# One-hot rows written one token and key at a time, and the low weight parts of the expert products' first factor made on VectorE

## The chip, the core and the metric

The kernel runs on one core of a Trainium2 chip. The metric is the time of one execution on the device in microseconds. A core has TensorE (PE in the profile, its weight loads PEld), VectorE (DVE), ScalarE (ACT), GpSimd (POOL) and the queue that starts the plain DMA transfers (SP).

## What is computed

The reference is a decoder trunk of two layers over 512 tokens of width 1024. Layer 0 mixes tokens with chunkwise retention, layer 1 with causal differential attention. After each mixer, with a layer norm on either side, stands a PEER feed-forward block, and the change lies in that block. There each of 8 heads picks the best 16 of 128x128 = 16384 experts for each token, and the token's result is a sum over these 128 experts:

```python
s1, i1 = lax.top_k(sc[:, :, 0], PEER_TOPK)
s2, i2 = lax.top_k(sc[:, :, 1], PEER_TOPK)
cand = (s1[..., :, None] + s2[..., None, :]).reshape(PEER_CHUNK, PEER_HEADS, ncand)
cidx = (i1[..., :, None] * PEER_N_KEYS + i2[..., None, :]).reshape(PEER_CHUNK, PEER_HEADS, ncand)
top, pos = lax.top_k(cand, PEER_TOPK)
idx = jnp.take_along_axis(cidx, pos, axis=-1).reshape(PEER_CHUNK, PEER_HEADS * PEER_TOPK)
gate = jax.nn.softmax(top, axis=-1).reshape(PEER_CHUNK, PEER_HEADS * PEER_TOPK)
u_e = jnp.take(u, idx, axis=0)
v_e = jnp.take(v, idx, axis=0)
act = jax.nn.gelu(jnp.einsum('ted,td->te', u_e, xc).astype(jnp.float32))
return jnp.einsum('te,ted->td', (gate * act).astype(v_e.dtype), v_e)
```

## The kernel before

Tokens stand in four blocks of 128. In the PEER block, `peer`, block 0 is done sparsely: for each of its 128 picks a gather on GpSimd's queue fetches one row of u (`sparse_u`, line 752) and later of v (`sparse_v`, line 765) for every token, and VectorE takes the dot product (line 754, tile `scr`) or the weighted sum (line 767). Blocks 1 to 3, 384 tokens, are done densely: all 16384 experts are computed, as 128 tiles `a` of 128 experts, and multiplied with a gate matrix that is zero where an expert was not picked.

Every float32 product with the wide weights is made of three products of rounded parts (`mm3`, lines 107 to 109). `wload` brings a weight tile of 128x1024 in (`wraw`, a ring of 9 buffers that the gathered rows share), ScalarE copies it to its high part `wh` (line 103), and the subtraction on line 104 makes the low part `wl`, on the engine that the caller names and on VectorE if it names none.

`u_tile` is the first product of a dense tile: 24 matmuls of 384 columns, then gelu on ScalarE into `uact`. Its low part is made on GpSimd. `v_prep` and `v_mm` are the second product: 18 matmuls of 512 columns. Their low parts, `wl` of v and `wwl`, are made on VectorE.

The gate matrix comes from `gmat`. For four tokens at a time it builds two sets of one-hot rows of 128 keys, `g_oh`, one of them weighted with the gate, and PE multiplies them (line 844). One instruction on VectorE compares the number row with the keys of the four tokens in bf16 (line 837, `g_eq`, 1024 columns), ScalarE copies one half of the result to float32 (line 839), and VectorE multiplies the other half with the gate (line 840, 512 columns). There are 96 such groups of four tokens to a layer. `gate_rows` (lines 814 to 824, and the transposes of line 820) prepares the keys of a block of tokens, and `topk_pairs` (lines 695 to 739, tiles `tk_...`) picks the experts.

In a layer the order is: queries and scores with the first pick (`topk_keys`); `topk_pairs` for blocks 0 and 1; then `gates()`, which interleaves the gate groups of blocks 1 to 3, the picking of blocks 2 and 3, 82 of the 128 first products (their `uact` is stored to memory by SP) and part of the sparse dot products; then all 128 second products, of which the first 82 read `uact` back and the last 46 make their first product there, four ahead. The sparse rows of v are gathered in this last part. Fixed numbers (`UT`, `DOTS`, `LAG`, `PC`, and the costs that `gmat` yields) set the interleaving in program order, and the build's scheduler then sets the order on each engine. Each engine runs its own list in order.

Of the kernel before, what the change touches and what calls it, by code (L numbers as in the profile page):

```python
# [19 lines left out]
F32 = mybir.dt.float32  # L20
F32R = mybir.dt.float32r
BF16 = mybir.dt.bfloat16
I32 = mybir.dt.int32
U32 = mybir.dt.uint32
AF = mybir.ActivationFunctionType
OP = mybir.AluOpType
# [3 lines left out]
P = 128  # L30
# [22 lines left out]
VB = 4  # L53
NG0 = 2
OHB = 4
EQB = 2
UT = 4.0
RING = 9
SB = 4
# [4 lines left out]
def build(tc, I, out):  # L64
    nc = tc.nc
    ctx = ExitStack()
    with ctx:
# [8 lines left out]
        def ct(name, shape, dt=F32):  # L76
            return const.tile(shape, dt, name=name)
# [2 lines left out]
        mhalf = ct("mhalf", [P, 16])  # L80
        nc.vector.memset(mhalf, -0.5)
        iota50 = ct("iota50", [P, NCAND, 16], BF16)
        iota4 = ct("iota4", [P, P, 4], BF16)

        X = [xp.tile([P, D], F32, name=f"x{t}") for t in range(TB)]
        XTH = xp.tile([P, KD, S], F32R, name="xth")
# [724 lines left out]
        def gate_rows(kp, idx, gate):  # L811

            ii = kp.tile([P, 2, P], I32, name="g_ii", tag="g_ii")
            nc.vector.tensor_scalar(out=ii[:, 0, :], in0=idx, scalar1=7, scalar2=None, op0=OP.arith_shift_right)
            nc.vector.tensor_scalar(out=ii[:, 1, :], in0=idx, scalar1=127, scalar2=None, op0=OP.bitwise_and)
            fi = kp.tile([P, 2, P], F32, name="g_if", tag="g_if")
            nc.vector.tensor_copy(out=fi, in_=ii)
            b = bank("rt")
            for i, src in enumerate((fi[:, 0, :], fi[:, 1, :], gate)):
                nc.tensor.transpose(b[:, i * P:i * P + P], src, ident)  # L820
            tr = kp.tile([P, 3, P], F32, name="g_tr", tag="g_tr", bufs=2)
            nc.vector.tensor_copy(out=tr.rearrange("p a b -> p (a b)"), in_=b[:, :3 * P])
            ks = kp.tile([P, 2, P], BF16, name="g_ks", tag="g_ks", bufs=2)
            nc.vector.tensor_copy(out=ks, in_=tr[:, 0:2, :])
            return tr, ks

        def gmat(kp, tr, ks, t0, gd, G0):

            for q in range(P // GT):
                st = kp.tile([P, P - GA * NG0, GT], F32, name="g_st", tag="g_st", bufs=2)  # L830
                for r in range(GT // 4):

                    eq = kp.tile([P, 2, P, 4], BF16, name="g_eq", tag="g_eq", bufs=EQB)
                    oh = kp.tile([P, 2, 4, P], F32, name="g_oh", tag="g_oh", bufs=OHB)
                    tk = q * GT + r * 4
                    ts = slice(tk, tk + 4)
                    nc.vector.tensor_tensor(out=eq, in0=iota4[:, None].to_broadcast([P, 2, P, 4]),
                                            in1=ks[:, :, None, ts].to_broadcast([P, 2, P, 4]), op=OP.is_equal)
                    nc.scalar.activation(oh[:, 1], eq[:, 1].rearrange("p a t -> p t a"), AF.Copy)
                    nc.vector.tensor_tensor(out=oh[:, 0], in0=eq[:, 0].rearrange("p a t -> p t a"),  # L840
                                            in1=tr[:, 2, ts].unsqueeze(2).to_broadcast([P, 4, P]), op=OP.mult)
                    b = bank("pj")
                    for i in range(4):
                        nc.tensor.matmul(b[:, i * P:i * P + P], oh[:, 1, i, :], oh[:, 0, i, :], start=True, stop=True)  # L844
                    b3 = b.rearrange("p (t a) -> p t a", t=4)
                    rs = slice(r * 4, r * 4 + 4)
                    nc.scalar.activation(st[:, :, rs].rearrange("p a t -> p t a"), b3[:, :, GA * NG0:], AF.Copy)
                    for i in range(NG0):
                        nc.scalar.activation(G0[i][:, t0 // GT + q, :, rs].rearrange("p a t -> p t a"),
                                             b3[:, :, GA * i:GA * i + GA], AF.Copy)  # L850
                nc.sync.dma_start(gd[t0 // GT + q], st.rearrange("p a t -> p (a t)"))
                yield 6.0

        def u_tile(dp, l, a, tag="mu"):
            uh, ul = wload(I[f"ut{l}"][a], nc.gpsimd)
            b = bank(tag)
            for k in range(KD):
                newest["mm"] = mm3(b[:, :DT], uh[:, k, :], ul[:, k, :], XTH[:, k, S - DT:], XTL[:, k, S - DT:], k == 0, k == KD - 1)
# [20 lines left out]
        def peer(l, norm, feed, prepare):  # L879
            with tc.tile_pool(name="sp", bufs=1) as sp, tc.tile_pool(name="dp", bufs=1) as dp:  # L880
# [6 lines left out]
                with tc.tile_pool(name="p1", bufs=1) as kp:  # L887
                    M = [kp.tile([P, 16, 16], F32, name=f"tk_m{t}") for t in range(TB)]
                    MI = [kp.tile([P, 16, 16], U32, name=f"tk_i{t}") for t in range(TB)]
                    with tc.tile_pool(name="pq", bufs=1) as qp:  # L890
                        scores(qp, M, MI, l, norm, feed)
                        if l == 0:
                            iota_f = qp.tile([P, P], F32, name="iota_f")
                            nc.sync.dma_start(iota_f, I["iota"])
                            nc.vector.tensor_copy(out=iota50,
                                                  in_=iota_f[:, :NCAND].unsqueeze(2).to_broadcast([P, NCAND, 16]))
                            nc.vector.tensor_copy(out=iota4, in_=iota_f.unsqueeze(2).to_broadcast([P, P, 4]))
                    with tc.tile_pool(name="tk", bufs=1) as tp:
                        def pairs(t, got):
                            idx = tp.tile([P, P], I32, name="tk_idx", tag="tk_idx", bufs=2)  # L900
# [4 lines left out]
                        def gates():  # L905
# [18 lines left out]
                            for t in range(1, TB):  # L924
                                now = nxt
                                more = pairs(t + 1, got) if t + 1 < TB else ()
                                for n, cost in enumerate(gmat(tp, *now, (t - 1) * P, gd, G0)):
                                    yield cost
                                    for c in (more if n == P // GT - 4 else itertools.islice(more, 2)):
                                        yield c  # L930
# [158 lines left out]
```

## Time and profile before

| | us |
|---|---|
| median of 3 runs (3371.23 to 3378.87) | 3378.38 |
| the profiled execution | 3379.12 |
| its span | 3377.4 |
| VectorE busy in it | 2614.1 |
| GpSimd busy in it | 1604.4 |
| ScalarE busy in it | 1395.6 |

The granted clock of TensorE was 0.982 of full speed over the span. Times in the profile are of one execution. A row by line gives, after the count, the busy time of the group, the mean duration of one instruction, and the idle time of the engine before them with what ended it. Records of neighbouring VectorE instructions overlap a little: the next one starts before the end of the last is recorded. A duration holds the time for which an instruction that was already issued is kept from running.

For the stretches that the text speaks of: the picking of blocks 0 and 1 runs from about 545 to 655 us in layer 0 and from 2160 to 2268 us in layer 1; the gate stretch from 655 to 1003 and from 2268 to 2598 us; the second products with stored first products from 1003 to 1352 and from 2598 to 2960 us; the last stretch, with first products made there, from 1352 to 1690 and from 2960 to 3315 us.

### The profile page before, as it was taken

The numbers are of one execution on the slowest core, as the hardware profiler recorded it, in microseconds if no ns is written. First come the engines' busy times: TensorE is split into PE (matmuls) and PEld (weight loads), VectorE is DVE, ScalarE is ACT, GpSimd is POOL, SyncE is SP. The second block draws the span as 40 slices with busy tenths as digits, with TensorE's granted clock in tenths as the row PEclk, the third lists the DMA queues.
The fourth block names the chain that finished last, engine by engine and source line by source line (L and its number), as shares of the span: only waits on it lengthen the run. The fifth ranks groups of instructions, "written<-read, shape, count | busy, mean of one in ns | idle before, by whom it ended". The sixth has DMA issues, their size and how long they took to land.

```text
span 3377.4 us, 47027 instructions
## 1 busy us (share of the span) xinstructions
PE 3223.7 (95%) x16666; PEld 2852.8 (84%) x16666; DVE 2614.1 (77%) x4593; ACT 1395.6 (41%) x2436; POOL 1604.4 (48%) x919
## 2 busy tenths in 40 slices
PE   9999999799999999999999999989999999998998
PEld 7888889799998887888888668989999888788887
DVE  4444459999878888999973565899987887898896
ACT  3233333356673333333333543335677333333232
POOL 1101335655562333778734423565555323377782
PEclk9999999899999999999999999989999999999999
DMA  5222223467789999899942202336678999988893
GB/s 210 87 83 83 89 94 129 144 216 242 234 313 364 354 338 343 318 331 343 327 157 92 69 26 94 129 131 225 227 243 296 363 355 339 360 314 321 314 327 146
DMA packets 312637, 774.38 MB, mean 229 GB/s; under 512 B 25936, under 2 KB 154320, under 8 KB 312400
## 3 DMA queue, kind: packets, MB, share of 16 engines
q1 hardware_dynamic: 238672, 502.89, 43.4%
q0 software_dynamic: 73728, 268.47, 22.1%
q8 instruction: 131, 2.15, 0.3%
q14 instruction: 106, 0.87, 0.1%
HBM read 692.88 MB, written 78.38 MB: 228 GB/s over the span
## 4 chain that ended last, share of the span: by engine, by line
PE 60%; DVE 14%; issue 10%; POOL 7%; DMA 6%; ACT 2%; POOLq 0%; SPq 0%; DVEq 0%; ACTq 0%
PE pj L108 11%; PE pj L107 11%; PE pj L109 11%; PE rt L108 5%; PE rt L107 4%; PE rt L109 4%; POOL vg L765 3%; POOL wl L104 3%; PE mu L109 3%; PE mu L107 3%; PE mu L108 3%; PE pj L844 2%; DMA wraw<-in_ut 2%; DMA ug<-in_u,idx 2%; DVE tk_idf L736 2%
## 5 line engine op out<-in xcount | busy, mean ns | idle before, releaser
L104 POOL TENSOR_TENSOR wl<-wraw,wh 128x1024 fp32r<-128x1024 f32 x316 | 836.0, 2650 | 631.2 <-ACT wh L103 601.4
L103 ACT ACTIVATE wh<-wraw 128x1024 fp32r<-128x1024 f32 x632 | 660.4, 1054 | 592.3 <-PE pj L109 107.0
L104 DVE TENSOR_TENSOR wl<-wraw,wh 128x1024 fp32r<-128x1024 f32 x316 | 422.6, 1339 | 194.7 <-ACT wh L103 184.3
L752 POOL DMA_INDIRECT ug<-in_u,idx x256 | 325.1, 1270 | 477.9 <-DVE act L754 229.6
L109 PE MATMUL mu<-xth,wl 128*128 128x384 f32 (+1 forms) x1424 | 483.0, 339 | 22.6 <-POOL wl L104 22.5
L107 PE MATMUL mu<-xth,wh 128*128 128x384 f32 (+1 forms) x1424 | 482.9, 339 | 13.8 <-ACT wh L103 11.7
L108 PE MATMUL mu<-xtl,wh 128*128 128x384 f32 (+1 forms) x1424 | 479.6, 337 | 0.0
L765 POOL DMA_INDIRECT vg<-in_v,idx x256 | 338.1, 1321 | 168.1 <-DVE x L767 70.4
L754 DVE CUSTOM_DVE_ANT_0 scr<-ug,x 128x1024 bf16<-128x1024 f32 x256 | 354.6, 1385 | 57.9 <-DMA ug<-in_u,idx 57.1
L108 PE MATMUL pj<-wl,wwh 128*128 128x512 f32 x1024 | 398.8, 390 | 0.4 <-DVE wl L104 0.4
L767 DVE SCALAR_TENSOR_TENSOR x<-vg,wgt,x 128x1024 f32<-128x1024 f32 x256 | 394.4, 1541 | 4.4 <-DMA vg<-in_v,idx 1.2
L109 PE MATMUL pj<-wh,wwl 128*128 128x512 f32 x1024 | 396.6, 389 | 0.0
L103 ACT ACTIVATE wwh<-w 128x384 fp32r<-128x384 f32 x256 | 134.0, 525 | 633.6 <-PE rt L108 273.5
L107 PE MATMUL pj<-wh,wwh 128*128 128x512 f32 x1024 | 339.5, 393 | 19.4 <-ACT wh L103 17.4
L109 PEld LDWEIGHTS mu<-xth,wl 128*128 128x128 f32 x1424 | 270.8, 190 | 32.8 <-POOL wl L104 30.9
L107 PEld LDWEIGHTS mu<-xth,wh 128*128 128x128 f32 x1424 | 271.8, 191 | 21.0 <-ACT wh L103 13.7
L108 PEld LDWEIGHTS mu<-xtl,wh 128*128 128x128 f32 x1424 | 271.2, 190 | 3.1
L104 DVE TENSOR_TENSOR wwl<-w,wwh 128x384 fp32r<-128x384 f32 x256 | 171.3, 670 | 115.6 <-ACT wwh L103 114.9
L107 PEld LDWEIGHTS pj<-wh,wwh 128*128 128x128 f32 x1024 | 191.0, 188 | 60.2 <-ACT wh L103 22.6
L107 PE MATMUL rt<-xth,wh 128*128 128x384 f32 (+1 forms) x688 | 232.4, 338 | 0.2
L108 PE MATMUL rt<-xtl,wh 128*128 128x384 f32 (+1 forms) x688 | 230.6, 335 | 0.4 <-DVE xtl L104 0.4
L109 PE MATMUL rt<-xth,wl 128*128 128x384 f32 (+1 forms) x688 | 230.1, 334 | 0.0
(242 smaller groups left out, 6545.4 us busy)
## 6 DMA issues: line engine op xcount, KB each, us to landing
wraw<-in_ut SPq DMA_DIRECT2D x256, 512.0 KB, 4.6
wraw<-in_v SPq DMA_DIRECT2D x256, 512.0 KB, 7.0
gd<-g_st SPq DMA_DIRECT2D x48, 896.0 KB, 4.6
gl<-gd SPq DMA_DIRECT2D x28, 1536.0 KB, 14.0
ad<-uact SPq DMA_DIRECT2D x164, 192.0 KB, 2.9
aact<-ad SPq DMA_DIRECT2D x164, 192.0 KB, 6.5
wraw<-in_w_in SPq DMA_DIRECT2D x48, 512.0 KB, 4.0
wraw<-in_peer_w_q SPq DMA_DIRECT2D x32, 512.0 KB, 4.1
```

The source lines that it names most:

```text
L103: nc.scalar.activation(h, src, AF.Copy)
L104: newest["low"] = (eng or nc.vector).tensor_tensor(out=l, in0=src, in1=h.bitcast(F32), op=OP.subtract)
L107: nc.tensor.matmul(o, ah, bh, start=start, stop=False)
L108: nc.tensor.matmul(o, ah, bl, start=False, stop=False)
L109: return nc.tensor.matmul(o, al, bh, start=False, stop=stop)
L736: nc.vector.reduce_sum(out=idf[:, hs, :], in_=ex.rearrange("p h c k -> p h k c"), axis=AX.X)
L752: nc.gpsimd.indirect_dma_start(out=u, out_offset=None, in_=I[f"u{l}"], in_offset=bass.IndirectOffsetOnAxis(ap=idx[:, j:j + 1], axis=0))
L754: nc.vector.tensor_tensor_reduce(out=scr, in0=u, in1=X[t], scale=1.0, scalar=0.0, op0=OP.mult, op1=OP.add, accum_out=act[:, j:j + 1])
L765: nc.gpsimd.indirect_dma_start(out=v, out_offset=None, in_=I[f"v{l}"], in_offset=bass.IndirectOffsetOnAxis(ap=idx[:, j:j + 1], axis=0))
L767: nc.vector.scalar_tensor_tensor(out=X[t], in0=v, scalar=w[:, j:j + 1], in1=X[t], op0=OP.mult, op1=OP.add)
L844: nc.tensor.matmul(b[:, i * P:i * P + P], oh[:, 1, i, :], oh[:, 0, i, :], start=True, stop=True)
```

## The change

Two edits. In `gmat`, the two comparing and multiplying instructions on VectorE and the copy on ScalarE go. In their place come eight instructions on VectorE for each four tokens, each over 128 float32 columns of one token and one key: the number row is compared with that token's key, given as an operand of one value for each partition, and for the first key also multiplied with the token's gate, a second such operand. The tiles `g_eq` and `g_ks` and the number row in bf16 go. In `u_tile`, the low part is made on VectorE in place of GpSimd, for all 128 tiles of a layer.

```diff
--- before.py
+++ after.py
@@ -53,7 +53,6 @@
 VB = 4
 NG0 = 2
 OHB = 4
-EQB = 2
 UT = 4.0
 RING = 9
 SB = 4
@@ -80,7 +79,7 @@
         mhalf = ct("mhalf", [P, 16])
         nc.vector.memset(mhalf, -0.5)
         iota50 = ct("iota50", [P, NCAND, 16], BF16)
-        iota4 = ct("iota4", [P, P, 4], BF16)
+        iota = ct("iota", [P, P])
 
         X = [xp.tile([P, D], F32, name=f"x{t}") for t in range(TB)]
         XTH = xp.tile([P, KD, S], F32R, name="xth")
@@ -820,25 +819,22 @@
                 nc.tensor.transpose(b[:, i * P:i * P + P], src, ident)
             tr = kp.tile([P, 3, P], F32, name="g_tr", tag="g_tr", bufs=2)
             nc.vector.tensor_copy(out=tr.rearrange("p a b -> p (a b)"), in_=b[:, :3 * P])
-            ks = kp.tile([P, 2, P], BF16, name="g_ks", tag="g_ks", bufs=2)
-            nc.vector.tensor_copy(out=ks, in_=tr[:, 0:2, :])
-            return tr, ks
-
-        def gmat(kp, tr, ks, t0, gd, G0):
+            return tr
+
+        def gmat(kp, tr, t0, gd, G0):
 
             for q in range(P // GT):
                 st = kp.tile([P, P - GA * NG0, GT], F32, name="g_st", tag="g_st", bufs=2)
                 for r in range(GT // 4):
 
-                    eq = kp.tile([P, 2, P, 4], BF16, name="g_eq", tag="g_eq", bufs=EQB)
                     oh = kp.tile([P, 2, 4, P], F32, name="g_oh", tag="g_oh", bufs=OHB)
                     tk = q * GT + r * 4
-                    ts = slice(tk, tk + 4)
-                    nc.vector.tensor_tensor(out=eq, in0=iota4[:, None].to_broadcast([P, 2, P, 4]),
-                                            in1=ks[:, :, None, ts].to_broadcast([P, 2, P, 4]), op=OP.is_equal)
-                    nc.scalar.activation(oh[:, 1], eq[:, 1].rearrange("p a t -> p t a"), AF.Copy)
-                    nc.vector.tensor_tensor(out=oh[:, 0], in0=eq[:, 0].rearrange("p a t -> p t a"),
-                                            in1=tr[:, 2, ts].unsqueeze(2).to_broadcast([P, 4, P]), op=OP.mult)
+                    for i in range(4):
+                        key1, key2, gate = [tr[:, x, tk + i:tk + i + 1] for x in range(3)]
+                        nc.vector.tensor_scalar(out=oh[:, 1, i, :], in0=iota, scalar1=key2, scalar2=None,
+                                                op0=OP.is_equal)
+                        nc.vector.tensor_scalar(out=oh[:, 0, i, :], in0=iota, scalar1=key1, scalar2=gate,
+                                                op0=OP.is_equal, op1=OP.mult)
                     b = bank("pj")
                     for i in range(4):
                         nc.tensor.matmul(b[:, i * P:i * P + P], oh[:, 1, i, :], oh[:, 0, i, :], start=True, stop=True)
@@ -852,7 +848,7 @@
                 yield 6.0
 
         def u_tile(dp, l, a, tag="mu"):
-            uh, ul = wload(I[f"ut{l}"][a], nc.gpsimd)
+            uh, ul = wload(I[f"ut{l}"][a])
             b = bank(tag)
             for k in range(KD):
                 newest["mm"] = mm3(b[:, :DT], uh[:, k, :], ul[:, k, :], XTH[:, k, S - DT:], XTL[:, k, S - DT:], k == 0, k == KD - 1)
@@ -890,11 +886,9 @@
                     with tc.tile_pool(name="pq", bufs=1) as qp:
                         scores(qp, M, MI, l, norm, feed)
                         if l == 0:
-                            iota_f = qp.tile([P, P], F32, name="iota_f")
-                            nc.sync.dma_start(iota_f, I["iota"])
+                            nc.sync.dma_start(iota, I["iota"])
                             nc.vector.tensor_copy(out=iota50,
-                                                  in_=iota_f[:, :NCAND].unsqueeze(2).to_broadcast([P, NCAND, 16]))
-                            nc.vector.tensor_copy(out=iota4, in_=iota_f.unsqueeze(2).to_broadcast([P, P, 4]))
+                                                  in_=iota[:, :NCAND].unsqueeze(2).to_broadcast([P, NCAND, 16]))
                     with tc.tile_pool(name="tk", bufs=1) as tp:
                         def pairs(t, got):
                             idx = tp.tile([P, P], I32, name="tk_idx", tag="tk_idx", bufs=2)
@@ -924,7 +918,7 @@
                             for t in range(1, TB):
                                 now = nxt
                                 more = pairs(t + 1, got) if t + 1 < TB else ()
-                                for n, cost in enumerate(gmat(tp, *now, (t - 1) * P, gd, G0)):
+                                for n, cost in enumerate(gmat(tp, now, (t - 1) * P, gd, G0)):
                                     yield cost
                                     for c in (more if n == P // GT - 4 else itertools.islice(more, 2)):
                                         yield c
```

The scheduler's order of the two programs differs from the end of the scores on. (Lines are one to seven lower in the kernel after.) On VectorE in the gate stretch, before, a pair of picking steps, two instructions of a gate group and a sparse dot product (`scr`) stand like this:

```order
L744 TENSOR_REDUCE tk_z<-tk_g 128x8
L840 TENSOR_TENSOR g_oh<-g_eq,g_tr 128x512
L745 RECIPROCAL tk_z<-tk_z 128x8
L837 TENSOR_TENSOR g_eq<-iota_76,g_ks 128x1024
L746 TENSOR_TENSOR tk_g<-tk_g,tk_z 128x128
L840 TENSOR_TENSOR g_oh<-g_eq,g_tr 128x512
L837 TENSOR_TENSOR g_eq<-iota_76,g_ks 128x1024
```

In the kernel after, VectorE's list in the gate stretch reads:

```order
L834 TENSOR_SCALAR g_oh<-iota,g_tr 128x128
L836 TENSOR_SCALAR g_oh<-iota,g_tr 128x128
L103 TENSOR_TENSOR wl<-wraw,wh 128x1024
L753 ISA scr,act_3191<-ug,x_77 128x1024
L753 ISA act_3191 128x1
L729 TENSOR_TENSOR tk_eq<-iota_75,tk_pb 128x1600
L103 TENSOR_TENSOR wl<-wraw,wh 128x1024 x2
```

The one-hot instructions now stand in runs of alternating kinds, and the low parts of the first products (`wl`) stand between them. Of a layer's 82 low parts that are made ahead of the second products, 50 stand between the first and the last one-hot instruction, 23 in the picking of blocks 0 and 1 and eight ahead of it.

On GpSimd the low parts go from its list: between the query weights' parts at a layer's start and the last norms, the 128 gathers of u rows and then the 128 of v rows stand there behind one another, where before the low parts stood between them.

On PE, before, the gate matmuls stand in fours at the start of the gate stretch, each four behind one wait for VectorE's and ScalarE's halves:

```order
L844 MATMUL pj<-g_oh 128x128 [waits DVE_49,Activation_49]
L844 MATMUL pj<-g_oh 128x128 x3
L109 MATMUL mu<-xth,wl 128x384
L107 MATMUL mu<-xth,wh 128x384
L108 MATMUL mu<-xtl,wh 128x384
```

After, they stand there one by one between the matmuls of the first products:

```order
L840 MATMUL pj<-g_oh 128x128 [waits DVE_49] x2
L106 MATMUL rt<-xth,wh 128x384
L840 MATMUL pj<-g_oh 128x128 [waits DVE_49]
L107 MATMUL rt<-xtl,wh 128x384
L840 MATMUL pj<-g_oh 128x128 [waits DVE_49]
L108 MATMUL rt<-xth,wl 128x384
```

Each of them waits for its own token's rows from VectorE, and the first products' matmuls behind it in the list stand behind that wait.

## Rows read from the trace of the kernel before

**Rows 1.** The page: span; busy time, share and instructions of each engine.

```profile
span 3377.4 us, 47027 instructions
...
PE 3223.7 (95%) x16666; PEld 2852.8 (84%) x16666; DVE 2614.1 (77%) x4593; ACT 1395.6 (41%) x2436; POOL 1604.4 (48%) x919
```

**Rows 2.** Windows: stretch, length, busy us (xinstructions) by engine, clock, DMA share, GB/s.

```profile
core 0: us, PE busy (x) PEld busy (x) DVE busy (x) ACT busy (x) POOL busy (x), PEclk, DMA share, GB/s
...
545.00:655.00 110.00, 93.81 (x540) 93.12 (x538) 109.77 (x379) 36.07 (x49) 76.64 (x29) 0.93 0.41 134
...
655.00:1003.00 348.00, 333.82 (x2155) 330.62 (x2156) 298.13 (x328) 231.85 (x507) 198.56 (x95) 0.99 0.71 244
...
1003.00:1352.00 349.00, 342.01 (x1512) 282.42 (x1511) 286.94 (x433) 124.72 (x172) 113.49 (x91) 1.00 0.98 350
...
1352.00:1690.00 338.00, 319.65 (x1576) 285.83 (x1575) 314.50 (x239) 112.07 (x151) 264.48 (x162) 0.98 0.92 330
...
2268.00:2598.00 330.00, 317.94 (x2054) 314.72 (x2055) 284.01 (x316) 220.71 (x487) 183.02 (x86) 0.98 0.69 236
...
2960.00:3315.00 355.00, 333.12 (x1624) 299.12 (x1623) 325.06 (x245) 116.52 (x158) 269.66 (x164) 0.97 0.90 322
```

**Rows 3.** Timeline of VectorE: start us, us, what.

```profile
667.87 0.98 DVE L730 TENSOR_TENSOR tk_eq<-iota,tk_pb 128x1600 bf16<-128x1600 bf16 x1
...
672.32 0.68 DVE L840 TENSOR_TENSOR g_oh<-g_eq,g_tr 128x512 f32<-128x512 bf16 x1
...
676.99 2.31 DVE L840 TENSOR_TENSOR g_oh<-g_eq,g_tr 128x512 f32<-128x512 bf16 x1
```

**Rows 4.** Timeline of GpSimd, same stretch.

```profile
672.63 6.12 POOL L104 TENSOR_TENSOR wl<-wraw,wh 128x1024 fp32r<-128x1024 f32 x2 [4.45 <-ACT wh L103]
```

**Rows 5.** Lines, VectorE, 655 to 1003 us: what xcount, busy us, mean ns, idle before.

```profile
L840 DVE TENSOR_TENSOR g_oh<-g_eq,g_tr 128x512 f32<-128x512 bf16 x96 | 86.9, 917 | 5.8 <-PE pj L844 3.8
...
L837 DVE TENSOR_TENSOR g_eq<-iota,g_ks 128x1024 bf16<-128x1024 bf16 x96 | 85.1, 905 | 11.6 <-ACT g_oh L839 10.8
...
L754 DVE CUSTOM_DVE_ANT_0 scr<-ug,x 128x1024 bf16<-128x1024 f32 x38 | 69.3, 1825 | 27.5 <-DMA ug<-in_u,idx 27.1 <-DVE act L754 0.3
...
L730 DVE TENSOR_TENSOR tk_eq<-iota,tk_pb 128x1600 bf16<-128x1600 bf16 x8 | 17.5, 2183 | 0.0
```

**Rows 6.** Lines, VectorE, 1352 to 1690 us.

```profile
L767 DVE SCALAR_TENSOR_TENSOR x<-vg,wgt,x 128x1024 f32<-128x1024 f32 x126 | 196.9, 1562 | 2.1 <-DMA vg<-in_v,idx 0.5
...
L104 DVE TENSOR_TENSOR wl<-wraw,wh 128x1024 fp32r<-128x1024 f32 x38 | 61.2, 1611 | 6.4 <-ACT wh L103 6.3
...
L866 DVE TENSOR_TENSOR w<-uact,gl 128x384 f32<-128x384 f32 x37 | 40.7, 1099 | 10.3 <-ACT uact L860 10.3
```

**Rows 7.** By line: xcount, duration ns min/median/max, first and last start, form.

```profile
L104 DVE TENSOR_TENSOR wl<-wraw,wh x316: 1207/1221/3934, 7.1 to 3348.0; 128x1024 fp32r<-128x1024 f32 x158
...
L767 DVE SCALAR_TENSOR_TENSOR x<-vg,wgt,x x256: 1268/1278/3954, 1349.7 to 3311.9; 128x1024 f32<-128x1024 f32 x128
...
L754 DVE CUSTOM_DVE_ANT_0 scr<-ug,x x256: 1203/1217/3474, 650.0 to 2956.6; 128x1024 bf16<-128x1024 f32 x128
...
L866 DVE TENSOR_TENSOR w<-uact,gl x92: 498/551/3348, 1333.5 to 3343.1; 128x384 f32<-128x384 f32 x92
```

**Rows 8.** Timeline of VectorE: a TENSOR_SCALAR over 128 columns and its follower.

```profile
642.24 0.21 DVE L697 TENSOR_SCALAR tk_f<-tk_f 128x128 f32<-128x128 f32 x1
...
642.38 0.28 DVE L817 CAST g_if<-g_ii 128x256 f32<-128x256 int32 x1
```

**Rows 9.** Lines by form: MAX8 over 128 columns.

```profile
L685 DVE MAX8 tk_m<-sc 128x8 f32<-128x128 f32 x256 | 58.1, 277 | 78.4 <-ACT sc L808 78.4
```

**Rows 10.** Waits, 655 to 1003 us: who <- whom, us in total, times, longest.

```profile
DVE scr L754 <- DMA ug<-in_u,idx: 27.1, 9, 7.4
...
PE rt L820 <- DVE tk_g L746: 13.2, 2, 12.4
```

**Rows 11.** Chain that ended last, 1352 to 1690 us, shares by line.

```profile
by line: issue 34.1%; POOL vg L765 19.8%; POOL wl L104 12.6%; DVE x L767 8.4%; DMA vg<-in_v,idx 5.3%; DMA wraw<-in_v 3.1%; PE mu L109 2.6%; PE mu L107 2.2%; PE mu L108 2.2%; DVE wl L104 1.7%; PE pj L108 1.4%; PE pj L109 1.4%; SPq L115 0.9%;
```

## Prediction

> **What bounds the kernel now.** The first thing to read is the share of each engine: PE is busy for 95% of the span, VectorE for 77% and GpSimd for 48% [rows 1]. A busy PE is the usual end of the argument, so I asked the windows by stage where PE is not busy and who else is full there [rows 2]. In the stretch with stored first products (1003 to 1352 us) PE is busy for 342.0 of 349 us at clock 1.00, and the memory moves 350 GB/s: nothing to win there, and it shows what a good stretch looks like. In the last stretch (1352 to 1690) PE has 319.7 of 338 us at clock 0.98, VectorE 314.5 (93%), GpSimd 264.5 (78%), and its twin in layer 1 is the same, 333.1 of 355 at 0.97. In the gate stretch (655 to 1003) PE has 333.8 of 348 and VectorE 298.1 (86%). While blocks 0 and 1 are picked (545 to 655), VectorE has 109.8 of 110 us and PE 93.8: there VectorE sets the pace alone.
>
> The chain of the last stretch says who holds it: the gathers on GpSimd 19.8%, the low parts on GpSimd 12.6%, gaps that nothing explains 34.1%, VectorE's sums on the gathered rows 8.4%, and hardly any PE [rows 11]. So GpSimd's list is the path there, and the change takes a third of the work from it.
>
> The third thing is a cost that no share shows. VectorE's busy time holds time in which it is kept from running. The second half of a gate group takes 0.68 us, and 2.31 us when it starts at 676.99, while GpSimd runs two low parts from 672.63 to 678.75 [rows 3, 4]. The median of VectorE's own low part is 1.22 us and its longest 3.93 [rows 7]. An instruction of VectorE with two inputs in the local memory stands still while GpSimd works on such inputs. [...]
>
> **The change part by part.** The sum is made against the profiled execution, 3379.1 us; the median of the runs is 3378.4, so no correction is needed.
>
> *Low parts of the first products, last stretch.* GpSimd loses about 39 low parts, VectorE gains them. What VectorE gets back: 126 sums with 1.562 in place of 1.279 us, 35.7 us; 38 low parts of v with 1.611 in place of 1.221, 14.8; 37 gate products with 1.099 in place of 0.551, 20.3 [rows 6, 7]. That is 71 us. What it takes on: 38 x 1.15 us (1.221 less the 0.07 by which records overlap, which rows 8 show: 0.21 long, the next one 0.14 later), 44 us. Its work falls from 314.5 to 287 us, 85% of the stretch, and GpSimd's to the gathers. What is late next is PE or the memory. At full clock PE's 319.7 us would be 313, and at the 98% share of the good stretch 320, a gain of 18 us; for layer 1 333.1 x 0.97 / 0.98 = 330, a gain of 25. The memory would have to move 330 x 338 / 320 = 349 GB/s, what the good stretch does [rows 2]. So up to 43 us over both layers; I take 40. Bounds: 0, if the first products wait in VectorE's list as they did in GpSimd's, and 44.
>
> *Low parts before the gate stretch.* Eight stand between the last scores' picks and 23 among the picks of blocks 0 and 1, where VectorE has no time left [rows 2]. 31 x 1.15 = 36 us a layer go onto the path. Against this, 23 low parts of GpSimd no longer hold VectorE there; each can hold it for up to 1.6 us (2.31 less 0.68), together up to 37. The gain and the loss are of one size; PE, too, has a tile more to do ahead of the wait for the gates (13.2 us [rows 10]). I take +7 us a layer, +14, with bounds of 0 and +36 a layer.
>
> *The one-hot rows.* Removed from VectorE in the gate stretch: 86.9 + 85.1 us of 298.1 [rows 5]. Of the 126 left, the sparse dot products hold 38 x (1.825 - 1.217) = 23 us of standing still, the picks' compare 8 x (2.183 - 0.980) = 10 [rows 3, 5, 7], which go: 93. Added: 50 low parts, 57 us. Added: 96 x 8 = 768 one-hot instructions. The trace has no instruction of this form. The nearest is a comparison-free TENSOR_SCALAR of float32 over 128 columns: the next one starts 0.14 us after it [rows 8]. An operand of one value for each partition is priced by two neighbours of 1024 columns, 1.279 with it and 1.221 without [rows 7]: 0.06 more. So 0.20 us, and 154 us a layer. [...] I take 0.20, since the nearest row is of the same operation and width. Together 93 + 57 + 154 = 304 us, and with the 27 us for which VectorE waits for gathered rows [rows 10] 332 of 348. In layer 1 the same steps give 284 - 172 - 33 + 57 + 154 = 290, with the waits 317 of 330. It fits, barely, and PE stays the bound. But PE now waits for each token and VectorE for each freed buffer, and with 5% of slack some of this shows: I take the 3.8 us that VectorE waits for PE's buffers now [rows 5] once more, +4 us a layer, +8. The copy on ScalarE costs nothing either way; it is busy for 232 of 348 us [rows 2].
>
> [...]
>
> The sum: 3379 - 40 + 14 + 8 = 3361 us.
>
> **The rivals.**
> 1. *VectorE becomes the bound of the gate stretch (slower).* Place: the one-hot runs. It decides from (348 - 27 - 93 - 57) / 768 = 0.22 us for one instruction. [...] For it speaks that no row shows a float32 compare with such operands, against it that rows 8 show two thirds of the time of rows 9 for the same width.
> 2. *Half price.* The faster rate holds but the second operand costs another 0.06: 0.23 on average, 23 us more a layer, less the slack, 17 in all. 3378, no change.
> 3. *The last stretch does not pay.* The memory or VectorE's list, in which a sum that waits for its gathered row now also holds the first products' low parts, takes GpSimd's place: 3401. Against it: VectorE waits 0.5 us for gathers there [rows 6].
> 4. *The relief is larger.* One-hots at 0.14, the pick stretch without loss, and PE gets back half of its 14 us of idle time in each gate stretch [rows 2]: 3379 - 43 - 14 = 3322.
> [...]
> That the change does nothing is no case: both engines' lists differ.
>
> **How the numbers follow.** Forecast 0.45, rivals 0.15, 0.10, 0.12, 0.13 and 0.05, in that order. This kernel's measurement can tell about 0.3%, 10 us, from no change. The forecast's own range is 3340 to 3380, three quarters of it below 3369. Faster: 0.34 + 0.13 + a little of the second rival, 0.49. Slower: rivals 1, 3 and 5, 0.31 with a rest of the second. The same: 0.20. Signs are divided, so the range reaches to both: 3318 takes in rival 4, 3434 the near end of rival 1.
>
> **What would show it.** In the profile after: a one-hot instruction's start to the next one's near 0.20 us; no VectorE instruction of two inputs above 1.6 us outside the attention part; the last stretch with PE at 98% and clock 1.00 and some 20 us shorter; the gate stretch within 10 us of its length, VectorE at 90% or more. A gate stretch longer by 30 us with PE waiting for the one-hots would make it wrong, as would a last stretch of unchanged length.

## The result and the profile after

The changed kernel takes 3336.9 us (median of four runs, 3335.7 to 3338.7) where the kernel before took 3377.9 beside it: a ratio of 0.9883, with an interval of 0.9866 to 0.9900. That is 41 us less. Forecast were 18 us less, so the sign was right and the size was less than half of what came.

In the page, the span, then busy time, share of the span and number of instructions for each engine (before: [rows 1]):

```profile
span 3333.6 us, 47872 instructions
...
PE 3225.8 (97%) x16666; PEld 2855.3 (86%) x16666; DVE 2625.5 (79%) x5994; ACT 1301.3 (39%) x2244; POOL 1009.0 (30%) x663
```

VectorE took over 256 low parts and has 1401 instructions more, and its busy time rose by only 11 us, although 256 low parts at their median of 1.22 us are 313. Something went out of it again, and the lines below show what: the standing still.

To compare stages I cut both spans at the same events: the first gate matmul, the first matmul of a second product, and the first matmul of a first product made in the last stretch.

| us | before | after | low parts alone |
|---|---|---|---|
| layer 0, up to the gate stretch | 665.0 | 665.6 | 668.3 |
| layer 0, gate stretch | 346.2 | 342.2 | 323.5 |
| layer 0, second products | 734.2 | 718.6 | 713.0 |
| of these the last stretch | 392.7 | 378.7 | 374.5 |
| layer 1, up to the gate stretch | 531.3 | 532.5 | 537.9 |
| layer 1, gate stretch | 347.2 | 343.0 | 322.5 |
| layer 1, second products | 738.7 | 716.9 | 714.9 |
| of these the last stretch | 398.9 | 375.5 | 376.4 |

(The last column is an experiment, told below. What is missing to the span is a tail of some 15 us. In the last column 22 matmuls of one first product stand right behind the gate stretch; the last stretch is counted there from the next first product, behind as many second-product matmuls, 1476, as in the other columns.) The last stretches give 37.4 us of the change's gain and the gate stretches 8.2.

The cuts do not enclose the same work. A layer's gate stretch holds 1378 matmuls of first products before, 1342 after and 1292 with the low parts alone, and in the kernel after one such matmul starts 0.17 us after the last (median). The 36 that are missing after stand ahead of the gates; of the 86 that are missing in the last column 64 stand ahead of the gates and 22 behind them. So the times of whole kernels carry the argument, and the stretches say where to look.

Windows of the kernel after, with the columns of [rows 2]: picking, gate stretch and last stretch of layer 0, then the last stretch of layer 1:

```profile
551.70:665.60 113.90, 104.69 (x578) 102.56 (x577) 113.15 (x379) 37.04 (x51) 24.09 (x9) 0.97 0.54 181
665.60:1007.80 342.20, 330.69 (x2119) 324.21 (x2118) 335.24 (x984) 186.78 (x413) 85.36 (x37) 0.99 0.69 241
1347.70:1726.40 378.70, 372.11 (x1844) 336.18 (x1843) 317.71 (x320) 129.37 (x176) 169.64 (x128) 0.99 0.89 321
...
2943.30:3318.80 375.50, 368.10 (x1836) 332.40 (x1835) 312.90 (x319) 125.59 (x171) 167.52 (x125) 1.00 0.86 311
```

In the last stretches PE is busy for 98%, and VectorE, though it makes 41 low parts more (87 in place of 46), has room. In the gate stretch it is the other way round: VectorE, the third busy column, has 335.2 of 342.2 us, 98%, and PE 97%. The chain that ended last, by line, first in the gate stretch and then in the last stretch of layer 0:

```profile
by line: PE pj L840 13.1%; DVE g_oh L836 12.6%; DVE g_oh L834 9.4%; PE mu L108 7.1%; PE mu L106 6.8%; PE mu L107 6.8%; DVE wl L103 6.6%; PE rt L108 5.7%; PE rt L107 5.6%; PE rt L106 5.6%; issue 5.2%; DVE tk_idf L735 4.3%; DVE scr L753 3.7%;
```

```profile
by line: PE mu L108 15.3%; PE mu L106 14.9%; PE mu L107 14.9%; PE pj L106 10.6%; PE pj L107 10.4%; PE pj L108 10.3%; PE rt L106 5.1%; PE rt L108 5.0%; PE rt L107 5.0%; DMA wraw<-in_ut 4.3%; DVE wl L103 1.0%; DVE x L766 1.0%; ACT wh L102 0.8
```

The last stretch has become a chain of matmuls; the gathers, GpSimd's low parts and the unexplained gaps of [rows 11] are gone. In the gate stretch the one-hot instructions (L834, L836) stand in the chain beside the matmuls that read them (L840).

By line, with the count, the shortest, median and longest duration in ns, and the first and last start (compare [rows 7]; lines are one lower):

```profile
L103 DVE TENSOR_TENSOR wl<-wraw,wh x572: 1174/1224/1691, 7.2 to 3304.2; 128x1024 fp32r<-128x1024 f32 x191
```

```profile
L766 DVE SCALAR_TENSOR_TENSOR x<-vg,wgt,x x256: 1272/1281/1353, 1344.6 to 3261.1; 128x1024 f32<-128x1024 f32 x128
```

```profile
L753 DVE CUSTOM_DVE_ANT_0 scr<-ug,x x256: 1212/1220/1326, 622.3 to 2936.2; 128x1024 bf16<-128x1024 f32 x128
```

The medians are those of before. The longest fell from 3.93 to 1.69 us, from 3.95 to 1.35 and from 3.47 to 1.33: these three kinds are not held for a whole instruction of GpSimd any more. A few others still are, beside the low parts of other weights that GpSimd kept. The product with the gates, whose median is 0.56 us, lasts up to 2.49, beside a low part on GpSimd of 2.40:

```profile
L862 DVE TENSOR_TENSOR w<-uact,gl x92: 545/558/2489, 1328.5 to 3299.3; 128x384 f32<-128x384 f32 x92
```

The timeline of VectorE shows the new instructions (start us, us, what):

```profile
706.59 0.29 DVE L834 TENSOR_SCALAR g_oh<-iota,g_tr 128x128 f32<-128x128 f32 x1
706.78 0.35 DVE L836 TENSOR_SCALAR g_oh<-iota,g_tr 128x128 f32<-128x128 f32 x1
707.04 0.29 DVE L834 TENSOR_SCALAR g_oh<-iota,g_tr 128x128 f32<-128x128 f32 x1
707.23 0.35 DVE L836 TENSOR_SCALAR g_oh<-iota,g_tr 128x128 f32<-128x128 f32 x1
```

Their price is the distance of the starts: 0.19 us with one operand per partition (L834), 0.26 with two (L836). Over a layer's gate stretch the means are 0.196 and 0.257, on average 0.226 us.

### The profile page after: what moved, and what is told of

The parts are those of the page before. It is cut to its first block, busy times and chain, and to the rows that moved or that the text cites. A ratio compares the mean times of both kernels' runs of the same rounds, so it can differ in the third digit from the quotient of the medians.

```text
span 3333.6 us, 47872 instructions
## 1 busy us (share of the span) xinstructions
PE 3225.8 (97%) x16666; PEld 2855.3 (86%) x16666; DVE 2625.5 (79%) x5994; ACT 1301.3 (39%) x2244; POOL 1009.0 (30%) x663
## 4 chain that ended last, share of the span: by engine, by line
PE 76%; DVE 17%; issue 3%; DMA 2%; ACT 1%; POOL 0%; POOLq 0%; SPq 0%; ACTq 0%; DVEq 0%
PE pj L106 13%; PE pj L107 13%; PE pj L108 12%; PE mu L108 6%; PE mu L106 5%; PE mu L107 5%; PE rt L106 5%; PE rt L107 5%; PE rt L108 5%; DVE wl L103 3%; PE pj L840 3%; DVE g_oh L836 2%; DVE tk_idf L735 2%; DVE g_oh L834 2%; DVE tk_ex L732 1%
## 5 line engine op out<-in xcount | busy, mean ns | idle before, releaser
L103 DVE TENSOR_TENSOR wl<-wraw,wh 128x1024 fp32r<-128x1024 f32 x572 | 696.9, 1232 | 208.9 <-ACT wh L102 207.3
L751 POOL DMA_INDIRECT ug<-in_u,idx x256 | 423.1, 1653 | 1210.6 <-DVE wl L103 662.6
L106 PE MATMUL pj<-wh,wwh 128*128 128x512 f32 x1024 | 350.7, 392 | 10.7 <-ACT wh L102 10.7
L766 DVE SCALAR_TENSOR_TENSOR x<-vg,wgt,x 128x1024 f32<-128x1024 f32 x256 | 328.7, 1284 | 3.7 <-DMA vg<-in_v,idx 0.2
L753 DVE CUSTOM_DVE_ANT_0 scr<-ug,x 128x1024 bf16<-128x1024 f32 x256 | 314.4, 1228 | 3.9 <-DMA ug<-in_u,idx 3.7
L836 DVE TENSOR_SCALAR g_oh<-iota,g_tr 128x128 f32<-128x128 f32 x768 | 286.2, 373 | 0.0
L103 DVE TENSOR_TENSOR wwl<-w,wwh 128x384 fp32r<-128x384 f32 x256 | 142.5, 559 | 130.8 <-ACT wwh L102 123.3
L834 DVE TENSOR_SCALAR g_oh<-iota,g_tr 128x128 f32<-128x128 f32 x768 | 239.4, 312 | 0.5 <-PE pj L840 0.5
L840 PE MATMUL pj<-g_oh 128*128 128x128 f32 x1536 | 233.8, 277 | 3.8 <-DVE g_oh L836 3.4
```

What stands on the lines that cost most here:

```text
L103: newest["low"] = (eng or nc.vector).tensor_tensor(out=l, in0=src, in1=h.bitcast(F32), op=OP.subtract)
L106: nc.tensor.matmul(o, ah, bh, start=start, stop=False)
L751: nc.gpsimd.indirect_dma_start(out=u, out_offset=None, in_=I[f"u{l}"], in_offset=bass.IndirectOffsetOnAxis(ap=idx[:, j:j + 1], axis=0))
L753: nc.vector.tensor_tensor_reduce(out=scr, in0=u, in1=X[t], scale=1.0, scalar=0.0, op0=OP.mult, op1=OP.add, accum_out=act[:, j:j + 1])
L766: nc.vector.scalar_tensor_tensor(out=X[t], in0=v, scalar=w[:, j:j + 1], in1=X[t], op0=OP.mult, op1=OP.add)
L834: nc.vector.tensor_scalar(out=oh[:, 1, i, :], in0=iota, scalar1=key2, scalar2=None, op0=OP.is_equal)
```

## The experiments

All are one edit away from the kernel after (the first is shown as its edit of the kernel before). Medians stand against the kernel before on the same chip (3377.9 us for the kernel after, 3375.1 for the next four rows, 3371.6 for the last four), and the differences below are made from these. So a row's time itself can be some 6 us off another row's.

| kernel | us | ratio to before, interval | against before | against after |
|---|---|---|---|---|
| after | 3336.9 | 0.9883, 0.9866 to 0.9900 | -41.0 | |
| low parts alone | 3302.1 | 0.9789, 0.9772 to 0.9805 | -73.0 | -32 |
| one-hot rows alone | 3437.8 | 1.0191, 1.0168 to 1.0214 | +62.8 | +104 |
| dead subtractions on GpSimd | 3670.9 | 1.0884, 1.0865 to 1.0903 | +295.8 | +337 |
| dead copies on GpSimd | 3470.5 | 1.0287, 1.0270 to 1.0305 | +95.5 | +136 |
| no gate operand | 3308.5 | 0.9814, 0.9796 to 0.9833 | -63.1 | -22 |
| more one-hot instructions | 3380.6 | 1.0027, 1.0017 to 1.0037 | +9.0 | +50 |
| last 46 low parts on GpSimd | 3368.2 | 0.9994, 0.9980 to 1.0008 | -3.4 | +38 |
| first 31 low parts on GpSimd | 3332.0 | 0.9887, 0.9871 to 0.9904 | -39.5 | +1.5 |

**The two edits apart.** First the low parts on VectorE with the gate groups of before:

```diff
-            uh, ul = wload(I[f"ut{l}"][a], nc.gpsimd)
+            uh, ul = wload(I[f"ut{l}"][a])
```

> The second edit alone: the low parts of the first products on VectorE, the gate groups as before (two instructions on VectorE, a copy on ScalarE). Theory H (the gain is VectorE no longer being held by GpSimd's low parts): the old gate instructions, no longer held, need 96 x 1.21 = 116 us a layer where the new ones need 174, so this kernel is as fast as the changed one or a little faster, 3322 to 3337 us, with the last stretches about 14 and 24 us shorter than before. Theory Q (the gain is only that PE and the gathers no longer stand behind low parts in GpSimd's list): the same last stretches, and the same time within 10 us, 3327 to 3347. Rival O (the one-hot edit carries the 4 us that each gate stretch gained, by taking ScalarE's copy out of the chain): 3343 to 3353.

Then the one-hot rows of after, with the low parts left on GpSimd:

```diff
-            uh, ul = wload(I[f"ut{l}"][a])
+            uh, ul = wload(I[f"ut{l}"][a], nc.gpsimd)
```

> The first edit alone: one-hot rows by eight instructions for four tokens, the low parts of the first products still on GpSimd. Theory H: the last stretches stay as before (394 and 399 us); in the gate stretch VectorE has 298 - 172 + 174 = 300 us of work plus being held by 50 low parts a layer, by as much as before or more, so 3375 to 3400. Theory Q: GpSimd's list is as before, so is the time: 3370 to 3385. Rival O: 3365 to 3372.

The low parts alone give 73 us, more than both edits together: this kernel, 3302.1 us, is the fastest of all here. The one-hot rows alone cost 63, and on top of the low parts 32. Both are further than any theory had said: theory H had the direction, and it ended at 3322 us for the one kernel and at 3400 for the other, so it priced the holding too low. The windows say where: the gate stretch of layer 0, with the low parts alone and then with the one-hot rows alone.

```profile
668.30:991.80 323.50, 313.55 (x2068) 312.53 (x2067) 277.64 (x381) 231.63 (x505) 60.05 (x38) 0.98 0.73 257
```

```profile
662.50:1043.90 381.40, 352.06 (x2165) 342.58 (x2163) 369.81 (x886) 187.02 (x418) 193.15 (x97) 0.97 0.67 226
```

The stretch of 346.2 us becomes 323.5 by the one edit and 381.4 by the other, which leaves the last stretches nearly as they were (392.0 and 394.6, before 392.7 and 398.9). With both it is 342.2. So the change's 4 us in this stretch are the sum of two large effects: the low parts take 23 us off (25 in layer 1), and the one-hot rows put 19 back (20). Part of both is work that moved over a cut: 86 matmuls at 0.17 us are 15 of the 23, and 50 of them, which come back with the one-hot rows, are 8.5 of the 19. The groups of VectorE in it, low parts alone (columns of [rows 5]):

```profile
L104 DVE TENSOR_TENSOR wl<-wraw,wh 128x1024 fp32r<-128x1024 f32 x58 | 70.8, 1225 | 11.4 <-ACT wh L103 11.3
L840 DVE TENSOR_TENSOR g_oh<-g_eq,g_tr 128x512 f32<-128x512 bf16 x94 | 62.9, 690 | 17.0 <-PE pj L844 17.0
L837 DVE TENSOR_TENSOR g_eq<-iota,g_ks 128x1024 bf16<-128x1024 bf16 x93 | 61.7, 690 | 5.5 <-ACT g_oh L839 5.4
L754 DVE CUSTOM_DVE_ANT_0 scr<-ug,x 128x1024 bf16<-128x1024 f32 x39 | 47.8, 1225 | 11.5 <-DMA ug<-in_u,idx 11.3
```

The two instructions of a gate group last 0.69 us each, where they lasted 0.917 and 0.905 [rows 5]. At 0.69 a layer's 192 of them are 132 us. So of the 172 us that they took before, 40 were standing still, and those go with GpSimd's low parts, whatever becomes of the groups. With the dot products (38 at 1.225 in place of 1.825 us, 23 us) this is 63 us in one stretch. Freed of its holding, a group of four tokens costs 2 x (0.69 - 0.07) = 1.24 us, and the eight new instructions cost 8 x 0.226 = 1.81: 0.57 us more, 55 us for 96 groups. VectorE's 277.6 us rise to 335.2, by 58.

Where PE's time in the shorter stretch goes: its idle time there fell only from 14.8 to 10.0 us. The rest is mostly the 86 matmuls. Those ahead of the gates are not free: with the low parts alone the time up to the gate stretch grew by 3.3 and 6.6 us, and the whole kernel still gained 73.

**Who bounds the gate stretch.** Two kernels move only the price of the one-hot rows. One leaves the gate operand out:

```diff
-                        nc.vector.tensor_scalar(out=oh[:, 0, i, :], in0=iota, scalar1=key1, scalar2=gate,
-                                                op0=OP.is_equal, op1=OP.mult)
+                        nc.vector.tensor_scalar(out=oh[:, 0, i, :], in0=iota, scalar1=key1, scalar2=None,
+                                                op0=OP.is_equal)
```

> The changed kernel with the gate operand and its multiplication taken out of the first key's one-hot instruction (the gate matrix is then unweighted). All 768 one-hot instructions of a layer then start 0.196 us apart where half of them took 0.256: 23 us a layer less on VectorE. Theory V (VectorE, 335 us busy in a gate stretch of 342, is the bound there): the gate stretches shrink by 19 to 23 us each until PE bounds them at the 323 us of the kernel with the second edit alone: 3295 to 3305. Rival P (the gate matmuls that stand one by one on PE and wait for each token are what costs 19 us a layer against the old groups): 3330 to 3340.

The other repeats one of the eight instructions of each group:

```diff
+                        if i == 3:
+                            nc.vector.tensor_scalar(out=oh[:, 0, i, :], in0=iota, scalar1=key1, scalar2=gate,
+                                                    op0=OP.is_equal, op1=OP.mult)
```

> The changed kernel with the first key's one-hot instruction written twice for one token in four: 96 more of 0.256 us a layer, 24.6 us. Theory V: all of it shows, 49 us over both layers, 3380 to 3392. Rival P: VectorE has 7 us free in the stretch and PE sets the length, so 17 us a layer at most and rather less: 3340 to 3370.

The gate stretch of layer 0 without the gate operand, and with the repeated instruction:

```profile
665.70:997.60 331.90, 324.61 (x2118) 321.10 (x2118) 314.04 (x985) 185.93 (x414) 63.91 (x38) 1.00 0.73 252
```

```profile
665.60:1035.40 369.80, 339.78 (x2119) 332.18 (x2117) 358.55 (x1079) 187.81 (x413) 70.68 (x38) 0.95 0.66 226
```

Without the operand both kinds have the same distance of starts, 0.196 and 0.197 us, so the operand alone costs 0.061, 23 us a layer, and the stretches get 10 and 9 us shorter, where theory V had said 19 to 23. With 96 instructions more, 24.7 us a layer at 0.257, they get 28 us longer and the kernel 50 us slower, the full price. Work added to VectorE there is paid in full, and work taken away in part: VectorE is the bound, and some 10 us below it lies the next one. That PE bounds the stretch, as the prediction had it, falls for the kernel after. Rival P falls too: PE waits there for the one-hot rows themselves for 1.5 us in layer 0, and for VectorE's low parts of the first products for 8.1. Theory V set its floor too low, and the counts of matmuls say why: without the operand VectorE is at 95% of the stretch and waits for PE's buffers in the line of the one-hots (12.0 us over both layers), PE is at 98%, and the 8 us that remain to the 323.5 of the low parts alone are as long as 50 matmuls more take at 0.17 us. So the next bound looks like PE, which no run here tests by itself.

**The last stretch by itself.** Its first products get their low parts from GpSimd again:

```diff
-            uh, ul = wload(I[f"ut{l}"][a])
+            uh, ul = wload(I[f"ut{l}"][a], nc.gpsimd if a >= 82 else None)
```

> The changed kernel with the low parts of the last 46 first products of a layer back on GpSimd, those of the 82 made ahead on VectorE. If the stretches are worth what each showed by itself, the last ones go back from 379 and 376 to 393 and 399 us and the gate stretches stay at 342: 3370 to 3378. If the last stretch's gain hangs on what the gate stretch does with the gathers (more sparse rows left over or fewer), 3337 to 3360.

The last stretches go back to 397.6 and 396.0 us, the gate stretches stay at 341.3 and 343.9, and 38 us are lost. That is the 37.4 us of the table above. The gain of this stretch belongs to its own 46 low parts. PE waited there for low parts that GpSimd made late, 7.2 us before and 5.7 in this run (layer 0); how the rest divides between GpSimd's full list and the holding of VectorE is not shown.

**The low parts ahead of the gate stretch.** Those that stand ahead of it or in the picks go back to GpSimd:

```diff
-            uh, ul = wload(I[f"ut{l}"][a])
+            uh, ul = wload(I[f"ut{l}"][a], nc.gpsimd if a < 31 else None)
```

> The changed kernel with the low parts of the first 31 first products of a layer back on GpSimd: those ahead of the picks of blocks 0 and 1 and among them. By the step of the prediction (the move costs 7 us a layer there) 3321 to 3327. By the kernel with the first edit alone, whose gate stretch begins 3.1 and 1.1 us earlier after its start, 3330 to 3337, no difference that can be measured.

The gate stretch starts 6.7 us earlier in layer 0 and 3.6 in layer 1, and then lasts 3.3 and 1.9 us longer: it holds 1389 matmuls of first products in place of 1342, and the 47 stand ahead of it in the kernel after. Against before both kernels gain the same, 39.5 and 41.0 us, which this measurement cannot tell apart. The cost that the prediction named is there, some 5 us a layer, but it comes with these 47 matmuls done ahead, and about half of it comes back in the gate stretch.

**The holding by itself.** For each first product GpSimd makes a result that nothing reads, first with two inputs in the local memory, then with one:

```diff
             uh, ul = wload(I[f"ut{l}"][a])
+            with behind("low"):
+                idle = dp.tile([P, KD, P], F32, name="idle", tag="idle")
+                nc.gpsimd.tensor_tensor(out=idle, in0=XTH[:, :, 0:P].bitcast(F32), in1=ul.bitcast(F32), op=OP.subtract)
```

> The changed kernel with one more instruction on GpSimd for each of the 256 first products: a subtraction of 128x1024 float32 of two tensors in the local memory, as long as the low part was, behind that product's low part, whose result nothing reads. Theory H: GpSimd holds VectorE again for up to 1.6 us each time, some 57 times in a gate stretch where VectorE is 98% busy, so the gate stretches grow by 30 us or more each and the last stretches lose half of their gain: 3400 to 3470. Theory Q: PE waits for none of it, only the gathers stand behind it: 3337 to 3355.

```diff
             uh, ul = wload(I[f"ut{l}"][a])
+            with behind("low"):
+                idle = dp.tile([P, KD, P], F32, name="idle", tag="idle")
+                nc.gpsimd.tensor_copy(out=idle, in_=ul.bitcast(F32))
```

> As the run with the dead subtraction on GpSimd, but a copy with one input of the same 128x1024. Theory H in its narrow form (only GpSimd instructions of two inputs hold VectorE): 3337 to 3350, and VectorE's medians and maxima as in the changed kernel. Theory H in its wide form (any GpSimd work on the local memory holds VectorE for as long as it lasts): between the changed kernel and the one with the dead subtraction, by the copy's length over 2.4 us, 3370 to 3430. Theory Q: 3337 to 3355.

The dead work on GpSimd (whole kernel, columns of [rows 5]), with two inputs and with one. The subtractions last 2.95 us on average, where the low parts that they stand for lasted 2.60 in the last stretch of layer 0 before:

```profile
L854 POOL TENSOR_TENSOR idle<-xth,wl 128x1024 f32<-128x1024 f32 x256 | 754.2, 2946 | 664.9 <-DVE wl L103 645.5 <-DVE tk_f L696 8.6 <-DVE tk_ci L708 5.4
```

```profile
L854 POOL COPY idle<-wl 128x1024 f32<-128x1024 f32 x256 | 384.7, 1503 | 738.7 <-DVE wl L103 725.7 <-DVE tk_f L696 8.7 <-DVE rs_t L184 3.0
```

Nothing reads what GpSimd makes there. Yet 754 us of subtractions cost 337 us and 385 us of copies cost 136, more than theory H's 3400 to 3470 and 3370 to 3430 us allowed; its narrow form and theory Q fall. Late gathers are not the reason. In the whole kernel with the subtractions VectorE waits for gathered rows for 0.4 us (who <- whom, us in total, times, longest), in the one with the copies for 0.7:

```profile
DVE scr L753 <- DMA ug<-in_u,idx: 0.4, 1, 0.4
```

It is busy, or held, for nearly all of the gate stretch (layer 0; two inputs, then one):

```profile
693.90:1139.80 445.90, 384.71 (x2118) 356.40 (x2117) 445.41 (x969) 188.80 (x413) 206.43 (x90) 0.92 0.55 182
```

```profile
669.80:1058.70 388.90, 357.12 (x2129) 340.81 (x2128) 386.80 (x978) 187.35 (x413) 135.53 (x94) 0.95 0.62 215
```

One-hot instructions beside them, by line (two inputs; then one input), and in the kernel with copies a reduction that reads one tensor:

```profile
L836 DVE TENSOR_SCALAR g_oh<-iota,g_tr x768: 289/336/3246, 688.8 to 2871.3; 128x128 f32<-128x128 f32 x192
```

```profile
L836 DVE TENSOR_SCALAR g_oh<-iota,g_tr x768: 291/336/1872, 666.5 to 2697.4; 128x128 f32<-128x128 f32 x192
```

```profile
L735 DVE TENSOR_REDUCE tk_idf<-tk_ex x32: 2824/2949/3025, 576.1 to 2554.1; 128x32 f32<-128x1600 f32 x32
```

A one-hot instruction of 0.34 us lasts up to 3.25 beside subtractions of 2.95 us, and up to 1.87 beside copies of 1.50: its own time and one whole instruction of GpSimd. The reduction is not held (2.82 to 3.03 us, in the kernel after 2.92 to 3.04, in the kernel before, beside low parts of 2.40 us on GpSimd, 2.91 to 3.02). That the relief comes from what GpSimd no longer does, and not from a better order on VectorE, is shown by this: the same 5994 instructions on VectorE, in nearly the order of the kernel after, lose the gain several times over when GpSimd's load is put back. What in the two engines makes one stand still for the other no view here shows.

## Why the prediction was right or wrong

**Low parts of the first products, last stretch: right.** Taken were 40 us, measured are 37.4, and the last 46 low parts put back cost 38. The share forecast for PE, 98%, is what the windows show, and VectorE's forecast 85% came out as 84% (317.7 of 378.7). The sums on gathered rows went from 1.562 to 1.284 us as reckoned. That GpSimd's list was the path there is borne out as far as PE waited for its low parts before, 7.2 us in layer 0 and 13.1 in layer 1.

**Low parts before the gate stretch: +14 us taken, +1.8 measured** (0.6 and 1.2 by the table). This term was mis-sized and makes 12 of the 26 us between forecast and result. The step put a gain and a loss of one size side by side and then took the loss a little larger. The loss exists (the first 31 put back start the gates earlier by 6.7 and 3.6 us), but the relief in the picks more than pays for it there: they got 4.6 us shorter in layer 0 (118.5 to 113.9) though VectorE makes 23 low parts more in them, with their GpSimd work down from 77 to 24 us.

**The one-hot rows: this is the step that failed.** It gave +8 us for both layers, measured are -8.2. That it missed by no more than 16 us is luck: the two halves of the change are worth -47 and +39 us in these stretches, and the step had neither. Two of the signs that it named came true all the same and could not show the error: the gate stretch stayed within 10 us of its length, and VectorE was above 90%. Three errors lie in it.

The first is what it took for fixed. It held VectorE's new work, 304 us, against a stretch of 348 us in which "PE stays the bound", and looked only for what would make it longer. In the kernel after VectorE is the bound, and what its relief is worth had no term in the sum: with the low parts alone the stretch is 323.5 us, 47 us less over both layers (some 30 of them work that moved over the cuts), although the prediction itself had counted 33 us of standing still there. PE's waits for the two halves of the one-hot rows fell with it, from 11.4 us to 1.8 in layer 0. What bounded the stretch before is not tested by itself.

The second is the book-keeping of the holding. "86.9 + 85.1 us" were put to the one-hot edit, with rows whose means, 917 and 905 ns, contain the holding that the other edit ends. At 690 ns they are 132 us, 119 without the overlap. Against the 154 us that the same paragraph gives to the new instructions, the edit loses on the prediction's own numbers, whose undisturbed row had 0.68 us. For both edits together the sum is none the worse for it, but it hides that one of them loses; two sums, one for each edit alone, would have shown it.

The third is the price. The step had 0.14 us without an operand and 0.06 for an operand, which fit what was measured, and then added only one operand to all instructions. Half of them have two: 0.20 and 0.26, mean 0.23; measured are 0.196, 0.257 and 0.226. That is 768 x 0.026 = 20 us a layer, more than the 16 us of slack that were said to be left.

Put right, the terms are -37 (last stretch), +2 (before the gates), -47 (gate stretches by the low parts) and +39 (gate stretches by the one-hot rows), together -43 of the 43.8 us by which the profiled spans differ. Those of the gate stretches are differences between the cuts, with the moved matmuls in them.

**The rivals.** What the first one said of the bound came about: VectorE became the bound of the gate stretch, at 0.226 us for one instruction, just above the 0.22 from which it was to decide. Its time did not. No run shows the price behind its end of the range, 3434 us: measured are 0.196 and 0.257 us, and that rival started from a stretch of 348 us in place of 323. The second had the right price for the same wrong start. The third (the last stretch does not pay) fell. The fourth came nearest, 3322 us, with a pick stretch without loss and 7 us less in each gate stretch (measured 4), but it rested on one-hots at 0.14 us. Of the fifth, which has 0.05 among the chances, no run shows that one-hots in runs keep GpSimd from its gathers. Longer gathers came, and cost nothing: the gathers of rows of u, by line, after,

```profile
L751 POOL DMA_INDIRECT ug<-in_u,idx x256: 932/1298/16627, 600.6 to 2917.3; - x128
```

last up to 16.6 us where the longest was 2.4 before, but VectorE's idle time for their rows in the gate stretch, 27.1 us before [rows 10], is now, by group,

```profile
L753 DVE CUSTOM_DVE_ANT_0 scr<-ug,x 128x1024 bf16<-128x1024 f32 x37 | 46.3, 1251 | 1.7 <-DMA ug<-in_u,idx 1.7
```

1.7 us. The likely reason is that GpSimd has no low parts between the gathers any more and runs ahead. The longest gather takes 7.2 us with the low parts alone and 4.4 with the one-hot rows alone.

**Few long instructions against many short ones.** One instruction over 1024 columns and one over 512 (1.24 us for four tokens) did, with a copy on ScalarE, the work of eight over 128 (1.81 us), and on top of the low parts the edit costs 32 us. That a fixed cost of each instruction is the reason is not shown, since types and operands change as well.

## What to carry to other kernels

Where one engine holds another, a recorded duration is work plus standing still (here 0.917 us on average, of which 0.69 are work): price each edit of a change by itself, with the median of the undisturbed instruction, and ask of each stretch how long it would be if the holding alone ended. Try taking elementwise work off GpSimd even where VectorE is nearly full and has to do it: here VectorE was busy for 86% of the gate stretch, and 1.2 us more on it ended up to 2.7 us of standing still at a time. And when many short instructions replace a few long ones, count the operands of each kind of them before the columns: over 128 columns they took 0.196 us with one and 0.257 with two.

## What was not expected of the hardware

A second operand of one value per partition, with its multiplication, costs 0.061 us over 128 columns, as much as the prediction took for a first: it priced the first at 0.06 us and left the second to a rival. The distance of starts over 128 float32 columns is 0.196 us with one and 0.257 with two, and 0.197 once the second is left out. For none there is one row, 0.14 us with another operation [rows 8].

A plain copy on GpSimd, one input, holds VectorE as well: 256 copies of 1.50 us that nothing reads cost 136 us, over a third of their own time. On VectorE's side, too, one tensor input is enough: the one-hots have one (up to 1.87 us beside these copies, 0.34 at the median), and so has a cast in the picks, which the kernel before already held for up to 2.36 us (after, its longest is 0.38):

```profile
L695 DVE CAST tk_f<-tk_i x8: 264/294/2364, 546.5 to 2252.3; 128x256 f32<-128x256 uint32 x8
```

From its rows the prediction had spoken of two inputs only, on either engine.
